# A rotary embedding that first writes sixteen short rows of zeros to its output, and stores five of eight blocks from GpSimd

## The chip, the cores and the metric

The kernel runs on one core of a Trainium2 chip. Such a core has five engines with their own instruction streams: TensorE (PE), VectorE (DVE), ScalarE (ACT), GpSimd (POOL) and SyncE (SP). Sixteen DMA engines move data between the device memory (HBM) and the on-chip memory (SBUF). The metric is device time in microseconds, the median of several runs. SBUF has 128 partitions, and a tile of "128x4096" is 4096 elements in each of them.

## The reference

A rotary position embedding over x of shape (8, 8, 1024, 64), float32, with one table of 32 frequencies, 1024 integer positions and a scale of 0.5:

```python
half = x.shape[-1] // 2
scaled_positions = positions * scale
angles = np.outer(scaled_positions, freqs)
cos = np.cos(angles)
sin = np.sin(angles)
x_first, x_second = (x[:, :, :, :half].copy(), x[:, :, :, half:].copy())
out_first = x_first * cos - x_second * sin
out_second = x_first * sin + x_second * cos
return np.concatenate([out_first, out_second], axis=-1).astype(np.float32)
```

x is 16.8 MB, and so is out. The cosine and sine tables are the same for all 64 heads.

## The kernel before

**Tiling.** The 64 heads are cut into 8 blocks of 8 heads. A block is a tile of 128 partitions by 4096 elements: 16 partitions to a head, 64 sequence positions to a partition, 64 elements to a position. In HBM a block is 2.10 MB in one piece; each partition is a row of 16 KB. The views `xv[u]` and `ov[u]` are block u of x and out.

**Loads.** Block 0 is loaded as float32 in two halves of columns, `X0f`: the left half by SP (line 63), the right half by ScalarE's queue (line 69). Ahead of that right half, ScalarE's queue issues two tiny loads, the positions `pos_i64` (line 66, 16 rows) and the frequencies `freq_row` (line 68, one row of 128 bytes). Blocks 1 to 7 are loaded by GpSimd (line 74), which converts to float16 on the way; between the first two of these it makes the selection matrix `sel`. All these issues come in the first six microseconds and wait for nothing but the start of the program.

**Tables.** VectorE sets two constants (`coef`, `quarter`). TensorE multiplies `coef` with `freq_row` to spread the scaled frequencies over the partitions (`cfreq`, line 93), and `sel` with the positions to spread these (`pos_ps`, line 101). VectorE forms their product `y` (line 108), takes off whole turns (lines 115 and 117), and ScalarE's sine gives `sinT` (line 121) and, from the absolute value, `cosT` (line 127), both in float16. ScalarE then converts block 0 to float16 (line 128).

**Main loop.** The blocks are worked in the order 1, 2, 0, 3, 4, 5, 6, 7. In each, VectorE does two multiplications of the whole tile (lines 136 and 137), one subtraction and one addition of half a tile (138 and 141); ScalarE converts the result to float32 into `OUT` (line 145), one of four buffers; then a store goes to `ov[u]` (line 146). The first four stores are issued by GpSimd, the last four by SP.

**Order.** Every operation of VectorE and ScalarE, and the loads of ScalarE's queue, are pinned to the order of the program text. Waits are set by a layer that follows tiles and tensors: an instruction waits for the last writer of what it reads, and for the users of what it overwrites. This also holds for `out` in HBM: a write to rows that an earlier DMA wrote waits for that DMA.

Of the kernel before, what the change touches and what calls it, by code (L numbers as in the profile page):

```python
# [1 line left out]

# [1 line left out]

# [4 lines left out]

FP32 = mybir.dt.float32
FP16 = mybir.dt.float16
I32 = mybir.dt.int32
AF = mybir.ActivationFunctionType
ALU = mybir.AluOpType

_MAGIC = 12582912.0
_TWO_PI_DN = float(np.float32(np.uint32(0x40C90FDA).view(np.float32)))

BUF_O = 4  # L20
BUF_P = 2


@with_exitstack
def kernel(
    ctx: ExitStack,
    tc: tile.TileContext,
    x: bass.AP,
    freqs: bass.AP,
    positions: bass.AP,  # L30
    scale: bass.AP,
    out: bass.AP,
):
    nc = tc.nc

    B, Hh, S, D = x.shape
    NBH = B * Hh
    half = D // 2
    P = nc.NUM_PARTITIONS
    HEADS = 8  # L40
    HP = P // HEADS
    K = S // HP
    N = K * D
    NU = NBH // HEADS
    assert S % HP == 0 and D == 2 * half and NBH % HEADS == 0

    fscale = float(scale)

    xv = x.rearrange("b h s d -> (b h s d)").rearrange("(u p n) -> u p n", p=P, n=N)
    ov = out.rearrange("b h s d -> (b h s d)").rearrange("(u p n) -> u p n", p=P, n=N)  # L50

    consts = ctx.enter_context(tc.tile_pool(name="consts", bufs=1))
    tmp = ctx.enter_context(tc.tile_pool(name="tmp", bufs=1))
    psum = ctx.enter_context(tc.tile_pool(name="psum", bufs=1, space=bass.MemoryType.PSUM))
    xin = ctx.enter_context(tc.tile_pool(name="xin", bufs=1))
    xout = ctx.enter_context(tc.tile_pool(name="xout", bufs=BUF_O))
    prods = ctx.enter_context(tc.tile_pool(name="prods", bufs=BUF_P))

    X0f = xin.tile([P, N], FP32, name="X0f")
    pin = tc.keep_in_program_order
    nc.sync.dma_start(out=X0f[:, : N // 2], in_=xv[0][:, : N // 2])

    pos_i64 = consts.tile([HP, K], positions.dtype)
    pin(nc.scalar.dma_start(out=pos_i64, in_=positions.rearrange("(q k) -> q k", k=K)))  # L66
    freq_row = consts.tile([1, half], FP32)
    pin(nc.scalar.dma_start(out=freq_row, in_=freqs[None, :]))
    pin(nc.scalar.dma_start(out=X0f[:, N // 2 :], in_=xv[0][:, N // 2 :]))

    X = [xin.tile([P, K, 2, half], FP16, name=f"X{u}") for u in range(NU)]

    def load(u):
        nc.gpsimd.dma_start(out=X[u].rearrange("p k h j -> p (k h j)"), in_=xv[u])  # L74


    sel = consts.tile([HP, HEADS, HP], FP32)
    load(1)
    nc.gpsimd.memset(sel, 0.0)
    nc.gpsimd.affine_select(  # L80
        out=sel, in_=sel, compare_op=ALU.not_equal, fill=1.0, base=0,
        pattern=[[0, HEADS], [-1, HP]], channel_multiplier=1,
    )
    for u in range(2, NU):
        load(u)


    coef = consts.tile([1, P], FP32)
    pin(nc.vector.memset(coef, fscale / (2.0 * np.pi)))  # L89
    quarter = consts.tile([P, 1], FP32)  # L90
    pin(nc.vector.memset(quarter, np.pi / 2.0))
    cfreq = psum.tile([P, half], FP32)
    nc.tensor.matmul(out=cfreq, lhsT=coef, rhs=freq_row, start=True, stop=True)  # L93

    pos_row = consts.tile([HP, K], FP32)
    pin(nc.vector.tensor_copy(  # L96
        out=pos_row,
        in_=pos_i64.bitcast(I32).rearrange("p (k t) -> p k t", t=2)[:, :, 0],
    ))
    pos_ps = psum.tile([P, K], FP32)  # L100
    nc.tensor.matmul(  # L101
        out=pos_ps, lhsT=sel.rearrange("q a b -> q (a b)"), rhs=pos_row, start=True, stop=True
    )
    posf = consts.tile([P, K], FP32)
    pin(nc.vector.tensor_copy(out=posf, in_=pos_ps))  # L105

    y = tmp.tile([P, K, half], FP32)
    pin(nc.vector.tensor_tensor(  # L108
        out=y,
        in0=posf.unsqueeze(2).broadcast_to((P, K, half)),  # L110
        in1=cfreq.unsqueeze(1).broadcast_to((P, K, half)),
        op=ALU.mult,
    ))
    m = tmp.tile([P, K, half], FP32)
    pin(nc.vector.tensor_scalar(out=m, in0=y, scalar1=_MAGIC, scalar2=None, op0=ALU.add))  # L115
    r = tmp.tile([P, K, half], FP32)
    pin(nc.vector.scalar_tensor_tensor(  # L117
        out=r, in0=m, scalar=_MAGIC, in1=y, op0=ALU.subtract, op1=ALU.subtract
    ))
    sinT = consts.tile([P, K, half], FP16)  # L120
    pin(nc.scalar.activation(out=sinT, in_=r, func=AF.Sin, bias=0.0, scale=-_TWO_PI_DN))  # L121
    ra = tmp.tile([P, K, half], FP32)
    pin(nc.vector.tensor_scalar(  # L123
        out=ra.bitcast(I32), in0=r.bitcast(I32), scalar1=0x7FFFFFFF, scalar2=None, op0=ALU.bitwise_and
    ))
    cosT = consts.tile([P, K, half], FP16)
    pin(nc.scalar.activation(out=cosT, in_=ra, func=AF.Sin, bias=quarter, scale=-_TWO_PI_DN))  # L127
    pin(nc.scalar.copy(out=X[0].rearrange("p k h j -> p (k h j)"), in_=X0f))  # L128

    cos_b = cosT.unsqueeze(2).broadcast_to((P, K, 2, half))  # L130
    sin_b = sinT.unsqueeze(2).broadcast_to((P, K, 2, half))


    for i, u in enumerate((1, 2, 0, *range(3, NU))):
        ps = prods.tile([P, K, 2, half], FP16, tag="ps")
        pin(nc.vector.tensor_tensor(out=ps, in0=X[u], in1=sin_b, op=ALU.mult))  # L136
        pin(nc.vector.tensor_tensor(out=X[u], in0=X[u], in1=cos_b, op=ALU.mult))  # L137
        pin(nc.vector.tensor_tensor(  # L138
            out=X[u][:, :, 0, :], in0=X[u][:, :, 0, :], in1=ps[:, :, 1, :], op=ALU.subtract
        ))  # L140
        pin(nc.vector.tensor_tensor(  # L141
            out=X[u][:, :, 1, :], in0=ps[:, :, 0, :], in1=X[u][:, :, 1, :], op=ALU.add
        ))
        OUT = xout.tile([P, N], FP32, tag="O")
        pin(nc.scalar.copy(out=OUT, in_=X[u].rearrange("p k h j -> p (k h j)")))  # L145
        (nc.gpsimd if i < NU // 2 else nc.sync).dma_start(out=ov[u], in_=OUT)  # L146


# [1 line left out]
_INS = ['x', 'freqs', 'positions', 'scale']  # L150
_OUTS = [((8, 8, 1024, 64), 'float32')]

_NUMBERS = {'scale': 0.5}


# [26 lines left out]
```

## Time and profile before

| what | value |
|---|---|
| median of four runs | 84.68 us (84.62 to 84.90) |
| the profiled execution's own time | 84.90 us |
| its span | 83.1 us |
| VectorE busy | 62.5 us (75%) |
| ScalarE busy | 37.4 us (45%) |
| GpSimd busy | 6.7 us (8%) |
| TensorE busy | 1.1 us (1%) |
| moved by the GpSimd queue (q0) | 15.73 MB in 1584 packets, 66.6% of the span of 16 engines |
| moved by the SP queue (q1) | 9.44 MB in 720 packets, 27.1% |
| moved by the ScalarE queue (q10) | 1.06 MB in 178 packets, 3.2% |
| HBM read and written | 16.79 MB and 16.78 MB, 404 GB/s over the span |

The profile is of one execution. The span runs from the first to the last event on the core; the execution's own time holds 1.8 us more. A page shows the busy share of each engine, then the span cut in 40 slices of 2.08 us with the busy share of each in tenths, then the DMA queues, and the chain of waits: the work that ended last, followed back step by step. The DMA row of the slices is the mean share of the 16 DMA engines, and the row under it is what they moved, counted by what they wrote. A load that converts from float32 to float16 therefore counts half of what it reads. The timeline lists instructions with start and duration in microseconds; in brackets is the idle time of the engine before it and what ended that. "ACTq", "SPq" and "POOLq" are instructions of an engine's own queue, such as the issue of a DMA.

### The profile page before, as it was taken

Reading aid. Unit: us, or ns where it says so; the run is one execution under the profiler, and the core shown is the slowest. Engines: PE = TensorE matmul, PEld = TensorE weight load, DVE = VectorE, ACT = ScalarE, POOL = GpSimd, SP = SyncE. Lnnn points to the kernel's source line nnn. Section 1 sums busy time; section 2 is a strip of 40 time slices with the busy share of each in tenths; the row PEclk is TensorE's granted clock in tenths of the full one; section 3 lists DMA queues with packets and bytes.
Section 4 is the critical chain, followed back from the end, with each engine's and each line's share of the span. In section 5 each row is a group of like instructions: output and inputs, shape, how many; then the busy total and the mean of one; then the engine's idle time right before and its main releaser. Section 6 shows DMA issues by size and latency. Waiting matters only on the chain.

```text
span 83.1 us, 154 instructions
## 1 busy us (share of the span) xinstructions
PE 1.1 (1%) x4; PEld 0.9 (1%) x4; DVE 62.5 (75%) x40; ACT 37.4 (45%) x12; POOL 6.7 (8%) x17
## 2 busy tenths in 40 slices
PE   0005000000000000000000000000000000000000
PEld 0004000000000000000000000000000000000000
DVE  0004999699999999999999999999999999200000
ACT  0600004999196079049319607904930960790000
POOL 4970000000002000200200200000000000000000
DMA  2799999999999999999999999999999999999990
GB/s 63 268 339 272 284 300 233 193 237 205 217 225 193 233 205 221 221 205 229 150 378 402 449 410 434 449 410 449 418 441 426 426 457 402 449 410 442 441 402 32
DMA packets 2482, 26.22 MB, mean 315 GB/s; under 512 B 290, under 2 KB 306, under 8 KB 306
## 3 DMA queue, kind: packets, MB, share of 16 engines
q0 software_dynamic: 1584, 15.73, 66.6%
q1 hardware_dynamic: 720, 9.44, 27.1%
q10 hardware_dynamic: 178, 1.06, 3.2%
HBM read 16.79 MB, written 16.78 MB: 404 GB/s over the span
## 4 chain that ended last, share of the span: by engine, by line
DVE 72%; ACT 7%; DMA 6%; DVEq 1%; PE 1%; issue 1%; ACTq 1%
DVE X L137 22%; DVE ps L136 21%; DVE X L138 12%; DVE X L141 10%; DMA freq_row<-in_freqs_dram 6%; ACT OUT L145 4%; DVE r L117 3%; DVE y L108 3%; ACT sinT L121 2%; DVE m L115 1%; DVEq L177 1%; PE cfreq L93 1%; PE pos_ps L101 1%; ACTq L66 0%; DVE posf L105 0%
## 5 line engine op out<-in xcount | busy, mean ns | idle before, releaser
L145 ACT CAST OUT<-X 128x4096 f32<-128x4096 f16 x8 | 28.8, 3605 | 25.0 <-DVE X L141 25.0
L136 DVE TENSOR_TENSOR ps<-X,sinT 128x4096 f16<-128x4096 f16 x8 | 18.3, 2285 | 0.7 <-ACT sinT L121 0.7
L137 DVE TENSOR_TENSOR X<-X,cosT 128x4096 f16<-128x4096 f16 x8 | 18.3, 2292 | 0.3
L138 DVE TENSOR_TENSOR X<-X,ps 128x2048 f16<-128x2048 f16 x8 | 9.8, 1225 | 0.3
L141 DVE TENSOR_TENSOR X<-ps,X 128x2048 f16<-128x2048 f16 x8 | 9.7, 1218 | 0.0
L121 ACT ACTIVATE sinT<-r 128x2048 f16<-128x2048 f32 x1 | 1.9, 1910 | 10.2 <-DVE r L117 10.2
L146 POOL DMA_DIRECT2D out_dram<-OUT x4 | 2.1, 534 | 40.1 <-ACT OUT L145 40.1
L74 POOL DMA_DIRECT2D X<-in_x_dram x7 | 3.9, 568 | 0.8 <-POOLq L163 0.8
L128 ACT CAST X<-X0f 128x4096 f16<-128x4096 f32 x1 | 3.6, 3589 | 0.0
L105 DVE COPY posf<-pos_ps 128x64 f32<-128x64 f32 x1 | 0.2, 224 | 3.6 <-PE pos_ps L101 3.6
L117 DVE SCALAR_TENSOR_TENSOR r<-m,y 128x2048 f32<-128x2048 f32 x1 | 2.3, 2293 | 0.0
L108 DVE TENSOR_TENSOR y<-posf,cfreq 128x2048 f32<-128x2048 f32 x1 | 2.3, 2286 | 0.0
L121 ACT ACT_TABLE_LOAD x1 | 1.3, 1283 | 2.1 <-issue 2.1
L96 DVE CAST pos_row<-pos_i 16x64 f32<-16x64 int32 x1 | 0.2, 181 | 2.7 <-DMA pos_i<-in_positions_dram 2.7
L127 ACT ACTIVATE cosT<-ra,quarter 128x2048 f16<-128x2048 f32 x1 | 2.0, 1987 | 0.0
L115 DVE TENSOR_SCALAR m<-y 128x2048 f32<-128x2048 f32 x1 | 1.2, 1226 | 0.0
L123 DVE TENSOR_SCALAR ra<-r 128x2048 int32<-128x2048 int32 x1 | 1.2, 1226 | 0.0
L89 DVE MEMSET coef<- 1x128 f32 x1 | 0.2, 165 | 0.8 <-PEq L163 0.8
L93 PE MATMUL cfreq<-freq_row,coef 1*128 1x32 f32 x2 | 0.6, 393 | 6.3 <-DMA freq_row<-in_freqs_dram 6.3
L101 PE MATMUL pos_ps<-pos_row,sel 16*128 16x64 f32 x2 | 0.7, 432 | 0.0
L93 PEld LDWEIGHTS cfreq<-freq_row,coef 1*128 1x128 f32 x2 | 0.5, 308 | 6.3 <-issue 6.3
L101 PEld LDWEIGHTS pos_ps<-pos_row,sel 16*128 16x128 f32 x2 | 0.5, 328 | 0.0
(7 smaller groups left out, 1.0 us busy)
## 6 DMA issues: line engine op xcount, KB each, us to landing
out_dram<-OUT POOLq DMA_DIRECT2D x4, 2048.0 KB, 19.9
out_dram<-OUT SPq DMA_DIRECT2D x4, 2048.0 KB, 10.5
X<-in_x_dram POOLq DMA_DIRECT2D x7, 1024.0 KB, 24.5
X0f<-in_x_dram SPq DMA_DIRECT2D x1, 1024.0 KB, 5.3
X0f<-in_x_dram ACTq DMA_DIRECT2D x1, 1024.0 KB, 11.9
pos_i<-in_positions_dram ACTq DMA_DIRECT2D x1, 8.0 KB, 2.9
freq_row<-in_freqs_dram ACTq DMA_DIRECT2D x1, 0.1 KB
```

The costliest lines, as they stand in the source:

```text
L74: nc.gpsimd.dma_start(out=X[u].rearrange("p k h j -> p (k h j)"), in_=xv[u])
L101: nc.tensor.matmul(out=pos_ps, lhsT=sel.rearrange("q a b -> q (a b)"), rhs=pos_row, start=True, stop=True)
L108: pin(nc.vector.tensor_tensor(out=y, in0=posf.unsqueeze(2).broadcast_to((P, K, half)), in1=cfreq.unsqueeze(1).broadcast_to((P, K, half)), ...
L117: pin(nc.vector.scalar_tensor_tensor(out=r, in0=m, scalar=_MAGIC, in1=y, op0=ALU.subtract, op1=ALU.subtract))
L121: pin(nc.scalar.activation(out=sinT, in_=r, func=AF.Sin, bias=0.0, scale=-_TWO_PI_DN))
L128: pin(nc.scalar.copy(out=X[0].rearrange("p k h j -> p (k h j)"), in_=X0f))
L136: pin(nc.vector.tensor_tensor(out=ps, in0=X[u], in1=sin_b, op=ALU.mult))
L137: pin(nc.vector.tensor_tensor(out=X[u], in0=X[u], in1=cos_b, op=ALU.mult))
L138: pin(nc.vector.tensor_tensor(out=X[u][:, :, 0, :], in0=X[u][:, :, 0, :], in1=ps[:, :, 1, :], op=ALU.subtract))
L141: pin(nc.vector.tensor_tensor(out=X[u][:, :, 1, :], in0=ps[:, :, 0, :], in1=X[u][:, :, 1, :], op=ALU.add))
L145: pin(nc.scalar.copy(out=OUT, in_=X[u].rearrange("p k h j -> p (k h j)")))
L146: (nc.gpsimd if i < NU // 2 else nc.sync).dma_start(out=ov[u], in_=OUT)
```

## The change

Two things are changed. First, VectorE sets a small tile `zero` (16 partitions by 128 float32) to zero ahead of its other constants, and ScalarE's queue, ahead of its loads, issues a DMA of this tile to `out`. There, `out` is cut into 16 equal pieces of 1.05 MB, and the first 512 bytes of each piece are written. So each block u holds two of these rows, at its beginning and in its middle. The stores of the results write these rows later, and the first store on each of the two store queues waits for the DMA of zeros. Second, of the eight stores GpSimd issues five instead of four, and SP three instead of four; the one that moves is that of block 4, the fifth in the order of work.

```diff
     nc.sync.dma_start(out=X0f[:, : N // 2], in_=xv[0][:, : N // 2])
+
+
+    R = 16
+    zero = consts.tile([R, 128], FP32)
+    pin(nc.vector.memset(zero, 0.0))
+    outr = out.rearrange("b h s d -> (b h s d)").rearrange("(r n) -> r n", r=R)
+    pin(nc.scalar.dma_start(out=outr[:, 0:128], in_=zero))
 
     pos_i64 = consts.tile([HP, K], positions.dtype)
     pin(nc.scalar.dma_start(out=pos_i64, in_=positions.rearrange("(q k) -> q k", k=K)))
...
         pin(nc.scalar.copy(out=OUT, in_=X[u].rearrange("p k h j -> p (k h j)")))
-        (nc.gpsimd if i < NU // 2 else nc.sync).dma_start(out=ov[u], in_=OUT)
+        (nc.gpsimd if i < 5 else nc.sync).dma_start(out=ov[u], in_=OUT)
```

Everything else stays, the order of VectorE's, ScalarE's and GpSimd's other instructions included.

## The prediction

> **What bounds the kernel now.** I read the page's slices first, then the timeline of the start, then the DMA queues stretch by stretch, then the end.
>
> ```profile
> span 83.1 us, 154 instructions
> DMA  2799999999999999999999999999999999999990
> GB/s 63 268 339 272 284 300 233 193 237 205 217 225 193 233 205 221 221 205 229 150 378 402 449 410 434 449 410 449 418 441 426 426 457 402 449 410 442 441 402 32
> DVE 72%; ACT 7%; DMA 6%; DVEq 1%; PE 1%; issue 1%; ACTq 1%
> ```
>
> The chain of waits calls this a VectorE kernel (72%). The DMA row says something else: the 16 engines are busy in every slice but the first two and the last. Until about 42 us they carry the loads (counted by the fp16 bytes written, so some 215 GB/s), then the stores at some 430 GB/s; a 2.10 MB store therefore takes 4.9 us. Two limits end almost together: DMA work without a hole, and the VectorE chain that releases the last store. What the change does to the end is decided by how far apart they are.
>
> The timeline of the first microseconds and its last issue (start, duration, instruction, idle before):
>
> ```profile
> 0.74 0.40 ACTq L66 DMA_DIRECT2D pos_i<-in_positions_dram  x1
> 0.74 0.37 SPq L63 DMA_DIRECT2D X0f<-in_x_dram  x1
> 0.82 0.17 DVE L89 MEMSET coef<- 1x128 f32 x1 [0.82 <-PEq L163]
> 1.17 0.53 ACTq L68 DMA_DIRECT2D freq_row<-in_freqs_dram  x1
> 1.25 0.67 POOL L74 DMA_DIRECT2D X<-in_x_dram  x1 [0.80 <-POOLq L163]
> 1.73 0.35 ACTq L69 DMA_DIRECT2D X0f<-in_x_dram  x1
> ...
> 3.70 0.18 DVE L96 CAST pos_row<-pos_i 16x64 f32<-16x64 int32 x1 [2.70 <-DMA pos_i<-in_positions_dram]
> 6.32 0.60 PE L93 MATMUL cfreq<-freq_row,coef 1*128 1x32 f32 x2 [6.32 <-DMA freq_row<-in_freqs_dram]
> ...
> 74.80 0.33 SPq L146 DMA_DIRECT2D out_dram<-OUT  x1
> ```
>
> To be seen: the 128 bytes of freq_row, issued at 1.17, release TensorE only at 6.32. From there VectorE hardly pauses until 71.1 and one ScalarE copy releases the last store at 74.80. A late freq_row moves all of this one to one.
>
> Why it takes 5 us stands in the queues' shares of two stretches, 3.5 to 5 us and 6 to 13 us (q1 is SP's queue, q10 ScalarE's, q0 GpSimd's):
>
> ```profile
> q1 hardware_dynamic: 73, 0.57, 90.9%
> q0 software_dynamic: 1, 0.01, 2.7%
> ...
> q0 software_dynamic: 136, 1.00, 68.1%
> q10 hardware_dynamic: 128, 0.93, 32.9%
> ```
>
> From 3.5 to 5 SP's half of X0f runs alone, though freq_row had been issued long before: what an engine has already taken from one queue goes first. From 6 to 13, q0 (the load of X1) and q10 (ScalarE's half of X0f) advance by about the same number of packets: they take turns, one packet each. An X1 packet costs 0.681 x 16 x 7 us over some 120 data packets, 0.63 us. So one small packet can wait 0.63 us for its turn.
>
> The same two habits later, in 53 to 57 us and 58 to 66 us:
>
> ```profile
> q0 software_dynamic: 112, 1.74, 101.3%
> ...
> q1 hardware_dynamic: 115, 1.88, 54.9%
> q0 software_dynamic: 102, 1.61, 46.8%
> ```
>
> SP's first store, issued at 54.03, moves nothing before 57; then both queues share evenly.
>
> Last, the DMA in four stretches of time (the last three numbers are clock, DMA share, GB/s), and the time to landing of the last store:
>
> ```profile
> 1.50:2.00 0.50, 0.00 (x0) 0.00 (x0) 0.00 (x0) 0.00 (x0) 0.50 (x2) 1.00 0.95 246
> ```
>
> ```profile
> 17.00:21.00 4.00, 0.00 (x0) 0.00 (x0) 3.86 (x3) 3.90 (x2) 0.00 (x0) 1.00 1.01 211
> 39.00:42.00 3.00, 0.00 (x0) 0.00 (x0) 2.97 (x2) 1.17 (x1) 0.53 (x1) 1.00 1.00 172
> 81.00:82.00 1.00, 0.00 (x0) 0.00 (x0) 0.00 (x0) 0.00 (x0) 0.00 (x0) 1.00 0.20 82
> ```
>
> ```profile
> out_dram<-OUT SPq DMA_DIRECT2D x1, 2048.0 KB, 7.4
> ```
>
> A DMA issued at 0.74 moves its first bytes between 1.5 and 2.0: 0.8 to 1.3 us. The last packets run into the stretch 81 to 82 and the store counts as landed at 74.80 + 7.4 = 82.2, a tail of some 0.4 us. On idle engines the last store would land at 74.80 + (0.8 to 1.3) + 4.9 + 0.4 = 80.9 to 81.4. It lands at 82.2 because earlier stores are ahead of it. **The slack** of the VectorE chain is the difference, 0.8 to 1.3 us; I take 1.0. A start that is late by d costs max(0, d - slack).
>
> **The change part by part.**
>
> *Memset of zero on VectorE.* 16x128; the nearest row is the memset of coef, 0.17 us. It puts coef back by 0.17, which is needed at 6.3: nothing, unless freq_row came 5 us sooner.
>
> *The zeros' DMA first on ScalarE's queue.* It waits for that memset, 0.82 + 0.17 = 0.99, against 0.74 for the first issue now, then issues in 0.35 to 0.53 (the three rows of ACTq). pos_i goes from 0.74 to 1.4-1.6, freq_row from 1.17 to 1.9-2.1, ScalarE's half of X0f from 1.73 to 2.4-2.6, the table load from 2.12 to about 2.9, done at 4.2 where sinT needs it at 13.6: hidden. The X0f half landed at 13.6 and its copy runs at 17.31: three microseconds of cover. Bytes: 8 KB, nothing against 33.6 MB.
>
> The issue delay of 0.75 us does not by itself move freq_row's landing, which waited behind SP's X0f until after 5 us anyway. Its place in the line does. Now the pos_i packets slip in among the first X0f packets (landed by 3.7), and freq_row is the first thing on its engine after SP's packets, ahead of X1, issued at 1.25. Afterwards a row of zeros with its semaphore write and a row of pos_i with its own go before it on the same queue, and freq_row is issued well after X1. Bounds for d: below, all of them still get in ahead of X1, 0.1 us (the nearest row is the landing of pos_i today, small packets among big ones at no visible cost). Above, each of the five packets up to freq_row and its semaphore write waits for an X1 packet, 5 x 0.63 = 3.1. The zeros are issued at about 1.0, before X1, so I let their two packets get through; the pos_i row and semaphore, freq_row and its semaphore then meet two or three X1 packets: 1.25 to 1.9, taken 1.6. pos_i lands late as well, but its cast (0.18) fits beside the cfreq matmul (0.60).
>
> On this step the Trainium skill, "DMA: Bandwidth & Descriptors", section Queues, rings and completion order, says an engine drains a whole packet of some 9 to 17 descriptors from one queue before it switches. By that, zeros, pos_i and freq_row would pass in one turn, d would be near 0.1 and the sum zero. The equal counts from 6 to 13 us, on a 0.63 and a 0.32 us packet, look like single turns to me, so I stay with them.
>
> *Waits on the zeros.* The first stores on GpSimd and SP now also wait for the zeros' landing, since they overwrite those rows. They are issued at 26.56 and about 61: the zeros land some 20 us before. Nothing.
>
> *The fifth store from SP to GpSimd.* The issue costs 0.53 instead of 0.33 us. GpSimd has nothing else then; its queue still holds 3.26 MB at 54, and SP's version did not move a byte before 57 anyway. Total bytes and order of release stay. The fourth store no longer shares with the fifth and lands earlier, which no one waits for: the copy into its buffer at 71.17 waits for VectorE. Bounds: +0.2 (issue, were the engines idle) and -0.2 by symmetry; taken 0.
>
> *A gain that the zeros could bring.* From 39 to 42, around the first store, 172 GB/s instead of 211: 3 x (1 - 172/211) = 0.55 us, with the dip just behind it some 0.65. If that is a cost of the first writes to out and the zeros pay it early, the DMA limit falls by 0.65. Bounds 0 and -0.65; I take 0, because the slow stretch begins while loads are still running, some 3 us ahead of the first store packets.
>
> *Sum.* 1.6 - 1.0 = +0.6. The profiled execution took 84.90 (span 83.1 and 1.8 around it), 0.22 above the median of the four runs, 84.68. So 85.5 against that execution, 85.3 against the median.
>
> **The rivals.** *The first-write stall goes and the start slips little.* For: the dip is real, and nothing before it writes to out. Against: its timing, and the queue order. The DMA limit gives -0.65, the chain 82.2 - 1.0 + d; to show more than 0.3%, 0.25 us (about what a measurement of this kernel tells from none), d must stay below some 0.75. 84.0 to 84.4.
>
> *The late start is hidden.* d of 0.6 to 1.2, one or two X1 packets, with the dip unchanged: 84.5 to 84.9. This is also the case in which the zeros do nothing. For: the slack is there. Against: the four small packets in front.
>
> *A long start.* All five packets take turns, or the zeros' write itself holds up its engine: d 2.5 to 3.1, +1.3 to +2.3, 86.0 to 87.0. Against: the zeros are issued before X1.
>
> **How the numbers follow.** Forecast case 0.42 (own range +0.3 to +1.1: 85.0 to 85.8); first-write gain 0.30; hidden 0.20; long start 0.08. Faster 0.30, same 0.20, slower 0.50. The range goes from the full gain, 84.0, to d = 2.5 with the smallest slack, +1.7, 86.4.
>
> **What would show it.** Right: freq_row releases TensorE at 7.5 to 8.3, the last store is issued at 76.1 to 76.7 and lands sooner after its issue than 7.4 us; a hole or dip in DMA just before it. The dip at 39 to 42 stays. Wrong: TensorE released before 7.0, or 39 to 42 at 211 GB/s with the stores done near 81.2, or the last store delayed by something on GpSimd's queue.

## The result, and the profile after

The changed kernel takes 84.78 us (median of 46 runs, 84.56 to 85.4), the kernel before 84.63 us (68 runs, 84.44 to 84.9). The ratio is 1.0024, 95% interval 1.0017 to 1.0032: slower, by 0.2 us (the medians alone differ by 0.15), where +0.6 was forecast. It lies inside the range, but at a third of the forecast size, and just below the 0.3%, 0.25 us, under which the forecast counted a change as none.

The page of the changed kernel, the lines that answer to those shown of before:

```profile
span 83.0 us, 159 instructions
DMA  2899999999999999999999999999999999999991
GB/s 39 304 312 273 273 308 245 221 209 217 213 217 217 213 217 209 221 213 221 150 332 442 434 427 434 411 442 442 427 434 419 450 419 434 434 427 442 411 442 47
DVE 73%; ACT 7%; DMA 6%; DVEq 1%; PE 1%; issue 1%; ACTq 0%
...
DVE X L144 22%; DVE ps L143 21%; DVE X L145 12%; DVE X L148 10%; DMA pos_i<-in_positions_dram 6%; ACT OUT L152 4%; DVE r L124 3%; DVE y L115 3%; ACT sinT L128 2%; DVE m L122 1%; DVEq L184 1%; PE cfreq L100 1%; PE pos_ps L108 1%; ACTq L70 0%
```

The DMA engines are still busy from end to end, and the dip is still there: slice 20 (39.4 to 41.5 us) has 150 GB/s in both kernels. The timeline of the start and of the last issue:

```profile
0.83 0.17 DVE L68 MEMSET zero<- 16x128 f32 x1 [0.83 <-PEq L170]
1.02 0.39 ACTq L70 DMA_DIRECT2D out_dram<-zero  x1
1.45 0.44 ACTq L73 DMA_DIRECT2D pos_i<-in_positions_dram  x1
1.92 0.53 ACTq L75 DMA_DIRECT2D freq_row<-in_freqs_dram  x1
...
6.31 0.18 DVE L103 CAST pos_row<-pos_i 16x64 f32<-16x64 int32 x1 [5.17 <-DMA pos_i<-in_positions_dram]
6.60 0.60 PE L100 MATMUL cfreq<-freq_row,coef 1*128 1x32 f32 x2 [6.60 <-DVE pos_row L103]
...
75.08 0.33 SPq L153 DMA_DIRECT2D out_dram<-OUT  x1
```

The bracket and the chain name pos_row and pos_i, but TensorE still waits for freq_row: in the trace freq_row landed at 6.47 and the cast of pos_row ended at 6.49, and in a second profile (after_again, below) TensorE started at 6.52, ahead of the end of that cast at 6.60.

The issues moved as forecast (freq_row 1.17 to 1.92, pos_i 0.74 to 1.45), and the whole chain came late one to one: TensorE 6.32 to 6.60, the last store 74.80 to 75.08. But this is 0.28 us only, and this execution is not even longer than the profiled one of before: 84.73 against 84.90 us. The profiled execution of before was the longest of its 68 runs. Two single profiles could not explain the result, so the parts were tried apart, and every run gave one more profile of a start.

### The profile page after: what moved, and what is told of

The parts are those of the page before. It is cut to its first block, busy times and chain, and to the rows that moved or that the text cites. A ratio compares the mean times of both kernels' runs of the same rounds, so it can differ in the third digit from the quotient of the medians.

```text
span 83.0 us, 159 instructions
## 1 busy us (share of the span) xinstructions
PE 1.1 (1%) x4; PEld 0.9 (1%) x4; DVE 62.7 (76%) x41; ACT 37.4 (45%) x12; POOL 7.2 (9%) x18
## 4 chain that ended last, share of the span: by engine, by line
DVE 73%; ACT 7%; DMA 6%; DVEq 1%; PE 1%; issue 1%; ACTq 0%
DVE X L144 22%; DVE ps L143 21%; DVE X L145 12%; DVE X L148 10%; DMA pos_i<-in_positions_dram 6%; ACT OUT L152 4%; DVE r L124 3%; DVE y L115 3%; ACT sinT L128 2%; DVE m L122 1%; DVEq L184 1%; PE cfreq L100 1%; PE pos_ps L108 1%; ACTq L70 0%; DVE posf L112 0%
## 5 line engine op out<-in xcount | busy, mean ns | idle before, releaser
L153 POOL DMA_DIRECT2D out_dram<-OUT x5 | 2.7, 533 | 46.8 <-ACT OUT L152 46.8
```

The costliest lines, as they stand in the source:

```text
L153: (nc.gpsimd if i < 5 else nc.sync).dma_start(out=ov[u], in_=OUT)
```

## The experiments

### The two parts by themselves, and the zeros elsewhere

Theory A: the late start is the price. B: the moved store is. C: the zeros' packets are, wherever they stand. Four kernels on one chip, before at 84.56 us beside them.

*zeros_only*, against the changed kernel:

```diff
-        (nc.gpsimd if i < 5 else nc.sync).dma_start(out=ov[u], in_=OUT)
+        (nc.gpsimd if i < NU // 2 else nc.sync).dma_start(out=ov[u], in_=OUT)
```

> The zeros first on ScalarE's queue, the stores split four and four as before. Theory A (the late start of freq_row and pos_i is the price): all of the change's +0.2 us is here, ratio 1.001 to 1.004, with freq_row releasing TensorE 0.2 us or more later than before's 6.32. Theory B (the store that moved is the price): no difference, ratio within 0.999 to 1.001.

Measured: 85.27 us, ratio 1.0080 (1.0066 to 1.0095). The zeros alone cost more than three times what the whole change costs.

*split_only*, against before:

```diff
-        (nc.gpsimd if i < NU // 2 else nc.sync).dma_start(out=ov[u], in_=OUT)
+        (nc.gpsimd if i < 5 else nc.sync).dma_start(out=ov[u], in_=OUT)
```

> No zeros; the fifth store goes from SP to GpSimd. Theory A: no difference, ratio within 0.999 to 1.001, the fourth store landing about 5 us sooner than before with no effect on the end. Theory B: +0.2 us, ratio 1.001 to 1.004.

Measured: 84.69 us, ratio 1.0015 (1.0005 to 1.0024). By itself the moved store gains nothing; beside the zeros it takes away 0.5 us. That fits none of A, B and C.

*zeros_last*: split four and four, the five lines of the zeros behind the loads.

```diff
     pin(nc.scalar.dma_start(out=X0f[:, N // 2 :], in_=xv[0][:, N // 2 :]))
+    R = 16
+    zero = consts.tile([R, 128], FP32)
+    pin(nc.vector.memset(zero, 0.0))
+    outr = out.rearrange("b h s d -> (b h s d)").rearrange("(r n) -> r n", r=R)
+    pin(nc.scalar.dma_start(out=outr[:, 0:128], in_=zero))
```

> The zeros behind the three loads on ScalarE's queue, split four and four. Theory A: no difference, since freq_row and pos_i are issued as before and land at the old times. Theory C (the sixteen extra short packets cost time in the DMA engines wherever they stand): +0.1 to +0.2 us here too.

Measured: 85.06 us, ratio 1.0053 (1.0041 to 1.0065), though TensorE starts at 5.46. A late start can't be the reason here.

*zeros_twice*: a second DMA of zeros ahead of the loads, split four and four.

```diff
     pin(nc.scalar.dma_start(out=outr[:, 0:128], in_=zero))
+    pin(nc.scalar.dma_start(out=outr[:, 128:256], in_=zero))
```

> Two DMAs of zeros (columns 0 to 127 and 128 to 255 of each piece) ahead of pos_i and freq_row, split four and four. Theory A: freq_row is issued another 0.45 us later and falls behind one or two packets of X1 more, TensorE starts 0.6 to 1.5 us later than before, and what exceeds the slack of about 1.0 us shows: ratio 1.002 to 1.010. Theory C: twice the price of one DMA, about +0.4 us, with no later start needed.

Measured: 86.14 us, ratio 1.0199 (1.0177 to 1.0222). TensorE starts at 8.36, two microseconds later than in the profile of before.

The place to look was the end. From these traces I took the landing of the last store (its issue and its time to landing) and the end of the span:

| run | last landing | end of span | between |
|---|---|---|---|
| before | 82.23 | 83.13 | 0.89 |
| the changed kernel | 82.06 | 82.97 | 0.90 |
| split_only | 82.19 | 83.09 | 0.90 |
| zeros_only | 82.17 | 83.51 | 1.33 |
| zeros_last | 81.86 | 83.18 | 1.32 |
| zeros_twice | 83.09 | 84.35 | 1.26 |

Three kernels need some 0.4 us more after their last landing. Their SP and ScalarE queues together issue nine DMAs (ten in zeros_twice); the others issue eight or fewer. The trace's records show what happens then. Eight completion semaphores serve these two queues, and the last store, as the ninth or tenth DMA, takes one that an early DMA had already used (in zeros_only that of SP's half of X0f). At the end of the program SP waits for all these semaphores in a fixed order, and each wait takes 0.06 us. In before the last store's semaphore is the last of them, and the waits for the other seven are over by then. In zeros_only it stands at the head: the wait for it ends at 82.19, and the seven others follow (82.25, 82.32 and so on to 82.62). In zeros_twice it stands second, and six follow.

### Nine DMAs without zeros, and zeros with eight

Theory D: it is this closing order. Before at 84.67 us.

*split_3_5*, against before:

```diff
-        (nc.gpsimd if i < NU // 2 else nc.sync).dma_start(out=ov[u], in_=OUT)
+        (nc.gpsimd if i < 3 else nc.sync).dma_start(out=ov[u], in_=OUT)
```

> No zeros; GpSimd issues three stores and SP five, so that SP and ScalarE together issue nine DMAs, as in the runs with zeros split four and four. Theory D (the ninth DMA of these two queues takes a completion semaphore that is already in use, which the closing sequence waits on first, so that seven more closing waits of 0.061 us each follow the last landing): the last landing as before, the span ends 1.33 us after it instead of 0.89, +0.43 us, ratio 1.004 to 1.006. Theory C (the zeros' packets cost): no difference, ratio within 0.999 to 1.002.

Measured: 85.07 us, ratio 1.0048 (1.0027 to 1.0068), without a zero being written. The waits of SP's queue at the end, first of before, then of split_3_5 (line, what it waited for, us in total, times, longest):

```profile
SPq L177 <- DMA out_dram<-OUT: 6.6, 2, 4.8
```

```profile
SPq L177 <- DMA out_dram<-OUT: 7.6, 1, 7.6
```

Before waits twice at the end, for the store before the last and, as the last thing, for the last. split_3_5 waits once for the last store and has the rest of the list still ahead; its span ends 1.32 us after the landing.

*zeros_last_5_3*: zeros_last with the five and three split, so eight DMAs.

```diff
-        (nc.gpsimd if i < NU // 2 else nc.sync).dma_start(out=ov[u], in_=OUT)
+        (nc.gpsimd if i < 5 else nc.sync).dma_start(out=ov[u], in_=OUT)
```

> The zeros behind the three loads on ScalarE's queue, stores split five and three: eight DMAs on SP and ScalarE. Theory D: the span ends 0.9 us after the last landing again and the 0.5 us of zeros_last are gone: ratio 0.999 to 1.002. Theory C: still 1.004 or more.

Measured: 84.62 us, ratio 0.9978 (0.9961 to 0.9996); the span ends 0.90 us after the landing. The price of zeros_last is gone. Its SP waits twice again, first zeros_last, then this run:

```profile
SPq L184 <- DMA out_dram<-OUT: 7.5, 1, 7.5
```

```profile
SPq L184 <- DMA out_dram<-OUT: 7.2, 2, 4.8
```

D holds in both directions: nine DMAs cost this without zeros, and zeros cost nothing with eight.

### How late the chain may be

*delay_1024*, against before:

```diff
+    idle = tmp.tile([P, 1024], FP32)
+    pin(nc.vector.memset(idle, 0.0))
     y = tmp.tile([P, K, half], FP32)
```

> Before with a memset of 128x1024 on VectorE behind posf, which does nothing but make the chain late by its duration d, 0.6 to 1.2 us. The slack theory: the end moves by d less the slack, where the slack is the landing of before's last store less 6.25 us (issue to landing when the engines wait for it, as measured with the zeros first) less its issue: 0.9 to 1.2. So +0 to +0.3 us, ratio 1.000 to 1.004, and the last store lands 6.2 to 6.6 us after its issue. Against it (every delay of the chain shows): the full d, ratio 1.007 to 1.014.

Measured: 84.74 us, ratio 0.9999 (0.9976 to 1.0022), the chain 0.9 us later behind TensorE. One sign did not come: the last store took 7.4 us to land, not 6.2 to 6.6, so it still met the stores ahead of it, and the slack was not used up. *delay_2048* has the memset twice; before at 84.59 us.

```diff
+    idle = tmp.tile([P, 1024], FP32)
+    pin(nc.vector.memset(idle, 0.0))
+    pin(nc.vector.memset(idle, 0.0))
     y = tmp.tile([P, K, half], FP32)
```

> Before with two memsets of 128x1024 on VectorE behind posf, so the chain is late by about 1.9 us (one of them made it 0.95 late at no measurable price). The slack theory: what exceeds a slack of 0.9 to 1.2 us shows, +0.4 to +1.0 us by where freq_row lands in the execution, ratio 1.004 to 1.012, and the last store lands 6.25 us after its issue. Against it: no price again (the DMA queue has more behind it than thought), or the full 1.9 us.

Measured: 85.18 us, ratio 1.0078 (1.0055 to 1.0100). From its timeline and its DMA issues:

```profile
5.65 0.60 PE L93 MATMUL cfreq<-freq_row,coef 1*128 1x32 f32 x2 [5.65 <-DMA freq_row<-in_freqs_dram]
...
76.21 0.33 SPq L149 DMA_DIRECT2D out_dram<-OUT  x1
```

```profile
out_dram<-OUT SPq DMA_DIRECT2D x1, 2048.0 KB, 6.3
```

The last store comes 2.1 us later behind TensorE than in before (70.56 against 68.48), and meets idle engines: 6.3 us from issue to landing, as in zeros_only. So an execution whose end the chain sets takes s + 68.48 + 6.26 + 0.90 + 1.77 = s + 77.4 us, with s the start of TensorE and 1.77 what lies around the span. With the 0.43 and 0.37 us of the longer closing this also gives zeros_only, 7.44 + 77.4 + 0.43 = 85.27, and zeros_twice, 8.36 + 77.4 + 0.37 = 86.13, as measured in their profiled executions. The slack is real and finite. But note s: 5.65 here, 5.56 in delay_1024. The ten profiles in which nothing stands ahead of pos_i and freq_row start at 5.35 to 6.32, mean 5.64. **The profiled execution of before, at 6.32, was the latest of all ten.** At a typical start the chain allows 83.0 us, and the slack is 1.6 us, not 1.0.

### Do the zeros give the stores anything?

zeros_last_5_3 looked slightly faster than before, so it was run again beside the split alone (before at 84.59 us).

> The zeros behind the three loads with five and three stores, a second time, beside the split alone on the same chip. If early zeros spare the stores something once they delay no load, this is faster than the split alone by 0.2 us or more, and the slow stretch at 39 to 42 us is shorter. If they do nothing, the two agree within 0.1 us, near 1.000.

> The split five and three alone, a second time: ratio 1.000 to 1.002 as in the first run if the moved store has a small price of its own, 0.999 to 1.001 if it has none.

Measured: 84.69 us both; ratios 1.0013 (0.9998 to 1.0028) and 1.0004 (0.9984 to 1.0023). Early zeros give nothing, and the first run's lead did not return. No version here beats before.

*no_first_three* leaves blocks 1, 2 and 0 of out unwritten; one execution:

```diff
-        (nc.gpsimd if i < NU // 2 else nc.sync).dma_start(out=ov[u], in_=OUT)
+        if i >= 3:
+            (nc.gpsimd if i < NU // 2 else nc.sync).dma_start(out=ov[u], in_=OUT)
```

> Before without the first three stores (blocks 1, 2 and 0 of out are left unwritten), so nothing waits behind the loads when these end at about 42 us, and the first store is issued at about 47. If the slow stretch at 39 to 42 us belongs to the beginning of writes to out, the loads end at about 42.2 without it (211 GB/s from 39 to 42), and the first store is slow later, if anything is. If it belongs to the last load, it stays at 39 to 42 us at 170 to 180 GB/s.

The same stretches as in before (clock, DMA share, GB/s at the end of each line), and the one behind its first store:

```profile
17.00:21.00 4.00, 0.00 (x0) 0.00 (x0) 3.86 (x4) 3.15 (x1) 0.00 (x0) 1.00 1.06 221
39.00:42.00 3.00, 0.00 (x0) 0.00 (x0) 2.97 (x3) 0.42 (x1) 0.00 (x0) 1.00 0.86 180
42.00:43.00 1.00, 0.00 (x0) 0.00 (x0) 1.00 (x2) 0.32 (x1) 0.00 (x0) 1.00 0.01 0
48.00:49.00 1.00, 0.00 (x0) 0.00 (x0) 1.00 (x2) 0.00 (x0) 0.00 (x0) 1.00 1.05 442
```

The line of before that the prediction calls "just behind" the dip:

```profile
42.00:43.00 1.00, 0.00 (x0) 0.00 (x0) 1.00 (x2) 0.00 (x0) 0.00 (x0) 1.00 1.04 385
```

The loads now end inside the stretch 39 to 42: a share of 0.86 at 180 GB/s is 209 GB/s while busy, the full rate, and nothing is left after 42. The last load lands 4.85 us after the one before it, as that one did; in the 17 profiles with all stores this takes 5.38 to 5.75 (before: 5.48, landing at 43.2 instead of 42.5). So the loss of some 0.65 us belongs to the passage from loads to stores that already stand behind them in the queue. It is not a fee for the first write to out: with writes first coming at 47, the stretch behind the first store has no such loss (442 GB/s from 48 to 49; this store took 6.56 us to land against 6.25 to 6.27 of SP's four, and 0.2 of the difference is GpSimd's longer issue). And the zeros of the changed kernel, some 37 us ahead, leave the dip where it was.

### What is left of the price

The changed kernel once more:

> The changed kernel once more, for a second profile. If its price is freq_row's turn behind packets of X1, which differs from one execution to the next, TensorE starts at 6.6 (no price), 7.2 to 7.4 (near the slack, +0.1 to +0.3) or about 8 (+0.6 to +0.9), and the times lie in as many clusters between 84.6 and 85.4; the span ends 0.9 us after the last landing in each.

Measured: 84.80 us, ratio 1.0005 (0.9988 to 1.0022); TensorE at 6.52, so no long execution. The twelve times, 84.64 to 85.18, form no clusters. By itself this run does not tell the change from none; its interval and the first one overlap from 1.0017 to 1.0022. Four further profiled executions:

> The changed kernel, one profiled execution out of four. If the price that is left is freq_row's turn, each execution's time follows from TensorE's start s: with s up to about 7.2 us the DMA queue sets the end, 84.5 to 84.9 us; beyond it the last store is issued at s + 68.48, lands 6.26 later, and the time is s + 77.4 (s = 7.4: 84.8 to 84.9; s = 8.0: 85.4). If an execution at 85.0 or more has s below 7.0, the price is something else.

> As for the first of the four: time = the larger of 84.5 to 84.9 and s + 77.4, with s the start of TensorE.

> As for the first of the four: time = the larger of 84.5 to 84.9 and s + 77.4, with s the start of TensorE.

> As for the first of the four: time = the larger of 84.5 to 84.9 and s + 77.4, with s the start of TensorE.

| profile of the changed kernel | TensorE starts (s) | s + 77.4 | last landing | time |
|---|---|---|---|---|
| first | 6.60 | 84.0 | 82.06 | 84.73 |
| after_again | 6.52 | 83.9 | 82.22 | 84.89 |
| look1 | 6.83 | 84.2 | 82.49 | 85.16 |
| look2 | 7.08 | 84.5 | 82.26 | 84.92 |
| look3 | 6.50 | 83.9 | 82.42 | 85.09 |
| look4 | 6.92 | 84.3 | 82.06 | 84.73 |

The rule expected for these four fell. The two long ones, look1 and look3, have s below 7.2, and s + 77.4 is 0.9 us and more short of their times. So the chain did not set their end; the DMA queue itself ended late. The page's line for SP's half of X0f says where it began (us to landing), first of look3, then of look4:

```profile
X0f<-in_x_dram SPq DMA_DIRECT2D x1, 1024.0 KB, 5.5
```

```profile
X0f<-in_x_dram SPq DMA_DIRECT2D x1, 1024.0 KB, 5.1
```

Since the engines are never idle afterwards, 0.4 us lost on the very first load are 0.4 us at the end: in all six profiles the last landing less this load's time is 76.9 to 77.0. The load's time is 5.0 to 5.3 in the ten profiles without zeros in front, and 5.1 to 5.5 in the eight with them (means 5.14 and 5.25). That would be half of the remaining 0.2 us, but the two groups overlap, and no run changed this alone. Whether the zeros slow that first load, or these two executions were chance, stays open. That single executions of the changed kernel with s above 7.2 add to it is possible too: zeros_only, whose start has the same issues, had one at 7.44, and there the chain set the end.

The longest times tell a little more: 10 of the 46 executions of the changed kernel took 85.0 us or more, and none of the 68 of before. But on the chip of after_again 5 of before's 35 did, against 2 of 12 of the changed kernel, and two profiles without zeros in front were as long, though the chain could not set their end: delay_1024 with 85.03 us (s = 5.56, with its 0.9 a chain limit of 83.8) and zeros_last_5_3 with 85.00 (s = 5.78). So such executions do not need the zeros; whether the zeros make them more frequent is not shown.

## Why the prediction was right or wrong

**What bounds the kernel: right.** DMA work and the VectorE chain end close together, and a late start costs only what exceeds the slack. The delays, zeros_twice and no_first_three (5.56 + 77.4 = 82.96, as measured) all obey it.

**The late start, d = 1.6: the first step that failed, by its size.** TensorE starts at 6.74 on average in six profiles of the changed kernel. That is 0.4 behind the 6.32 from which d was counted, and 1.1 behind the 5.64 of the ten others. As argued, the zeros, pos_i and freq_row queue up behind SP's X0f: in the first profile the zeros landed at 6.1, pos_i at 6.3 and freq_row at 6.5. But the sum let the row of pos_i, freq_row and their semaphore writes meet two or three packets of X1, and the traces' packet records show one or two. In the six profiles and in zeros_only the last row of pos_i starts 0.34 us after the last packet of SP's X0f does, which takes 0.31 itself: pos_i waits for no packet of X1. The semaphore write of freq_row starts 0.61 us after its 128 bytes, one X1 packet (0.63), where the ten profiles without zeros in front have 0.01 to 0.02. In zeros_only the 128 bytes themselves come late as well (6.37, against 5.45 to 6.03 in the six). Two zero DMAs, with which pos_i does fall behind X1, gave 2.7.

By the rule of the Trainium skill, "DMA: Bandwidth & Descriptors", section Queues, rings and completion order, that an engine drains a packet of some 9 to 17 descriptors before it switches, the prediction's estimate of d was near 0.1; its own bound, a turn for each packet, was 3.1. This case's traces lie between: zeros and pos_i pass without a turn of X1, freq_row's semaphore write does not.

**The slack, 0.8 to 1.3, taken 1.0: the second step that failed.** The estimate of 80.9 to 81.4 for a landing on idle engines was good (74.80 + 6.26 = 81.06, a slack of 1.17 for that execution). But the profiled execution had a freq_row later than any of the nine others, and a time 0.27 us above the median of all runs. For the usual start the slack is 1.6. So the sum was not 1.6 - 1.0 = +0.6 but 1.1 - 1.6, below zero: hidden. Either term put right alone would have brought the sum down to +0.1 or to 0. The rival "the late start is hidden" (d of 0.6 to 1.2, 84.5 to 84.9) describes what happened: d was 1.1, and 84.78 lies within its bounds. What the measured +0.2 consists of is not shown; the first load may account for half of it.

**The moved store, taken 0: right alone, wrong in company.** Alone it is 1.0015 and 1.0004. That agrees with what the Trainium skill, "DMA: Bandwidth & Descriptors", section Issuing engines are not separate DMA queues, says: the queues share the same 16 engines, so spreading stores over them gains no bandwidth. But beside the zeros it is worth 0.5 us, because it keeps the two hardware queues at eight DMAs. The prediction asked what waits on each DMA and not how many completion semaphores there are, and so it missed the closing order altogether. That its 0 came out was luck: the diff held the debt and its repayment.

**The waits of the first stores on the zeros, taken 0: right.** The zeros landed at about 6, the first store was issued at 26.8.

**The gain from early writes, taken 0 with a chance of 0.30: right, and for the reason given.** The slow stretch (39 to 42) begins before the first store's packets, which start at 42.0 in the trace of before, and it goes away when no store is queued.

**The marks.** TensorE at 7.5 to 8.3, the last store at 76.1 to 76.7 and a hole ahead of it were the marks for the forecast; 6.50 to 7.08, 75.0 to 75.6 and no hole came. The last store did land sooner than 7.4 us after its issue (6.65 to 7.39), and "the dip stays" came. Of the marks against the forecast, "TensorE released before 7.0" came in five of the six profiles. (One small slip in the sums: the rival "a long start" begins at 2.5 - 1.3 = +1.2, not at +1.3.)

## What to carry to other kernels

A slack between two limits that end together must come from more than one execution: a start that jitters by a microsecond moves the slack by as much. Count the DMAs of a kernel by queue before and after a change: here the ninth on two queues with eight completion semaphores put the last store at the head of the closing waits, for 0.4 us; an edit that looks neutral (a store on another queue) can be there to pay for that. And where DMA engines are busy from end to end, ask of the first load how long it took: in the six profiles of the changed kernel nothing later made up for it.

## What was not expected of the hardware

- The closing waits of SP: 0.06 us each, 0.43 us for the seven that follow when the last store's semaphore heads the list. Of a kernel of 84.6 us that is 0.5%, and it appears in no group, no busy share and no chain.
- The landing of one 128-byte load moved the start of the chain by up to a microsecond (5.35 to 6.32 us) between ten executions of programs with the same first issues. It did not set the time of the latest: 6.32 + 77.4 = 83.7, and that execution took 84.90.
- Loads with stores queued behind them lose 0.5 to 0.9 us on the passage from one to the other (the last load lands 5.38 to 5.75 us after the one before it, in 17 profiles); with an empty queue behind them they lose nothing (4.85, one profile).
